# End states of a recurrent unit in one VectorE copy, (a+1) multiplied in ahead of the square root, and ten constant products for four

## The chip, the cores and the metric

The kernel runs on one core of a Trainium2 chip. The metric is the device time of one execution in microseconds, as the median of several runs. Five engines work side by side, each through its own list of instructions in order: TensorE (PE; the loading of its weights is PEld), VectorE (DVE), ScalarE (ACT), GpSimd (POOL) and SyncE (SP, which only issues transfers here). They wait for each other at semaphores.

## The reference

One step of a two-layer backbone over 512 latent and 128 context tokens with 1024 channels. Layer 0 mixes tokens by attention, layer 1 by a bidirectional gated linear recurrence; a SwiGLU feed-forward block follows each. The change touches the recurrence only. For each channel and each direction:

```python
def _rglru_coeffs(xc, w_a, b_a, w_i, b_i, lam):
    ...
    r = jax.nn.sigmoid(jnp.einsum('btnk,nkj->btnj', xb, w_a).reshape(B, T, D) + b_a)
    i = jax.nn.sigmoid(jnp.einsum('btnk,nkj->btnj', xb, w_i).reshape(B, T, D) + b_i)
    log_a = -LRU_C * r * jax.nn.softplus(-lam.astype(jnp.float32))
    a = jnp.exp(log_a)
    b = jnp.sqrt(-jnp.expm1(2.0 * log_a)) * (i * xc)

def _linear_scan(a, b, h0, reverse):
    def step(h, ab):
        a_t, b_t = ab
        h = a_t * h + b_t
        return h, h
```

`xc` is a width-4 convolution over the tokens. The latent scans start from cached states, the context scans from zero. The sum of the forward and the backward states is multiplied by a GeLU gate and goes through the projection `lru_w_out`. The end states of the context scans, one number for each channel and direction, are an output of their own (`new_state_h`).

## The kernel before

Channels lie on the 128 partitions, tokens along the free dimension; 1024 channels make eight blocks f = 0 to 7 of 128. Large products are made in three passes (high part by high part, high by low, low by high: L228, L229, L230 in `some`), each weight tile being split into a high part (`whi`) and a low one (`wlo`, the subtraction of L183 on DVE). In this stage the high parts of the input weights come by a transfer that POOL issues (L179), and DVE can subtract once it has landed.

The recurrent unit is the stage between the two feed-forward blocks, from about 867 to 1014 us. For block f it goes through four functions:

- `lru_a`: the convolution (L1293 on ACT, three L1295 on DVE, into `xc`), four products with the recurrence weights into PSUM tiles `gp` (L1305), four tanh of them on ACT (L1306), giving `tr` for r and `ti` for i, each of 2 directions x 643 tokens; then ti = (ti + 1) * xc (L1307, DVE).
- `lru_b`: from tr, for each direction d, the decay a (L1317, an exponential on ACT) and a tanh that replaces tr (L1318, ACT). Of the new tr the square root is taken (L1319, ACT, both directions at once, after a change of the activation table, L1284, 1.28 us). Then on DVE tr = (a + 1) * tr (L1320) and ti = ti * tr (L1321). ti now holds b.
- `lru_c`: four scans on DVE (L1330; latent and context in each direction), which turn ti into the states h. After each direction POOL copies the one end state of the context scan, a column of h, into the tile `st` (L1332), sixteen copies in all. Then forward and backward states are added on DVE (L1337, L1338).
- `lru_d`: times the gate `gl` (L1343, DVE), the cast to the high part `yhi` (L1348, ACT; named `big` in the profile) and the low part `ylo` (L1350, DVE). For the last block, f = 7, these three are done in two halves.

Beside these, `lru_gate` makes the gates: products on PE, copied out by L1358, or put through GeLU (L1362) straight from PSUM, which frees that PSUM bank for PE's next product.

The stages of different blocks are interleaved: in round t the program writes `lru_a(t)`, `lru_b(t-1)`, `lru_c(t-2)`, `lru_d(t-2)`. On each engine a planner then sets the order: it takes the instructions in the order in which a model of the timeline finds them ready, so that a change of one instruction moves others. On ACT, `turn` chains the calls that need a certain activation table, so that their order is that of the program.

After the stage, `project_halves` multiplies by `lru_w_out`. Five partial products over blocks 0 to 4 are made ahead (L228 to L230), blocks 5, 6, 7 are added as they come (L1052 for yhi, L1054 for ylo), and between block 6 and block 7 `keep` puts products of constants into a PSUM tile that nobody reads (L211, tile `at`): four of 128 x 128. Each shows as two records in the profile. Past block 7 come the remaining five products of the projection, whose weights (`raw` from `in_wlo`) are loaded while the residual `x` is read back from memory (L1371).

Of the kernel before, what the change touches and what calls it, by code (L numbers as in the profile page):

```python
# [12 lines left out]
ALU = mybir.AluOpType  # L13
# [4 lines left out]
KT = D // P  # L18
# [16 lines left out]
LW = 643  # L35
NLT = 10
C0 = 515
# [89 lines left out]
class _Step:  # L127
# [908 lines left out]
    def project_halves(self, w, hi, lo, gk, key, xd):  # L1036
        def out(f, t0, t1, ps):
            self.residual(f, t0, t1, ps, G, True)
            self.nc.sync.dma_start(xd[f * P:f * P + P, t0:t1], self.x[:, f, t0:t1])
        G = self.need(self.gcols, gk)  # L1040
        us = [self.unit(w[f], "m") for f in range(3)]
        early = [(f, t0, t1) for f in range(3) for c, (t0, t1) in enumerate(CH) if c == 0 or f < KT - DEH]
        pss = [(self.ps("mx") if j % 2 else self.pg(False))[:, 0:HT] for j in range(len(early))]
        for (f, t0, t1), ps in zip(early, pss):
            self.some(us[f], hi, lo, t0, t1, ps, range(KT - 3))
        turns = sorted(zip(early, pss), key=lambda e: e[0][1])
        for k in range(KT - 3, KT):
            if k == KT - 1:
                self.keep(self.ps("at"), 4)
            for (f, t0, t1), ps in turns:  # L1050
                for part in us[f]:
                    self.done = self.nc.tensor.matmul(ps, part[:, k], hi[:, k, t0:t1], start=False, stop=False).ins  # L1052
            for (f, t0, t1), ps in turns:
                self.done = self.nc.tensor.matmul(ps, us[f][0][:, k], lo[:, k, t0:t1], start=False, stop=(k == KT - 1)).ins  # L1054
                if k == KT - 1:
                    out(f, t0, t1, ps)
        for f in range(3, KT):
            us.append(self.unit(w[f], "mx"[f % 2]))
            out(f, *CH[0], self.chunk(us[f], hi, lo, *CH[0]))
        self.rt = self.t([P, NTOK], F32, "r", 2)  # L1060
        for c, (t0, t1) in enumerate(CH):
            for f in range(KT - DEH, KT) if c else ():
                out(f, t0, t1, self.chunk(us[f], hi, lo, t0, t1))
                j = f - KT + DEH
                for k in range(max(0, 2 * j - 2), 2 * j) if f < KT - 1 else ():
                    self.first_half(k, key)
            self.stat(t0, t1)
            self.nc.scalar.copy(self.rt[:, t0:t1], self.r[0][:, 0:t1 - t0])
# [241 lines left out]
    def lru_b(self, f, lt, tr, ti):  # L1310
        nc = self.nc
        a = lt()
        nc.vector.tensor_scalar(tr, tr, -1.0, None, ALU.max)
        for d in range(2):
            p2 = self.sp2[:, d * KT + f:d * KT + f + 1]
            n4 = self.sm4[:, d * KT + f:d * KT + f + 1]
            self.turn(AF.Exp, lambda: nc.scalar.activation(a[:, d], tr[:, d], AF.Exp, scale=n4, bias=n4))  # L1317
            self.turn(AF.Exp, lambda: nc.scalar.activation(tr[:, d], tr[:, d], AF.Tanh, scale=p2, bias=p2))  # L1318
        self.turn(AF.Sqrt, lambda: nc.scalar.activation(tr, tr, AF.Sqrt, scale=0.25))  # L1319
        nc.vector.scalar_tensor_tensor(tr, a, 1.0, tr, ALU.add, ALU.mult)  # L1320
        nc.vector.tensor_tensor(ti, ti, tr, ALU.mult)  # L1321
        return a, ti

    def lru_c(self, f, a, h):
        nc = self.nc
        for d in range(2):
            st = self.st[:, d * KT + f:d * KT + f + 1]
            for sl, init in ((slice(0, NLAT), self.col(f"h{d}", f)), (slice(C0, LW), 0.0)):
                hv, av = [t[:, d, sl] if d == 0 else t[:, d, sl][:, ::-1] for t in (h, a)]
                nc.vector.tensor_tensor_scan(hv, av, hv, init, ALU.mult, ALU.add)  # L1330
            e = LW - 1 if d == 0 else C0
            nc.gpsimd.tensor_copy(st, h[:, d, e:e + 1])  # L1332
        y = a[:, 0, 0:NTOK]
        fn, bn = [h[:, d, 0:NLAT].rearrange("p (r c) -> p c r", r=ROWS) for d in range(2)]
        for c0, c1, q0 in ((56, 64, 0), (0, 56, 64)):
            yv = y[:, q0:q0 + (c1 - c0) * ROWS].rearrange("p (c r) -> p c r", r=ROWS)
            nc.vector.tensor_tensor(yv, fn[:, c0:c1], bn[:, c0:c1], ALU.add)  # L1337
        nc.vector.tensor_tensor(y[:, NLAT:NTOK], h[:, 0, C0:LW], h[:, 1, C0:LW], ALU.add)  # L1338
        return y
# [183 lines left out]
```

## Time and profile before

| | |
|---|---|
| Time, median of 3 runs | 1512.68 us (1512.1 to 1513.39) |
| The profiled execution's own time | 1511.01 us |
| Its span, first to last instruction | 1509.2 us |
| PE busy | 1483.2 us, 98% of the span |
| DVE busy | 1062.7 us, 70% |
| ACT busy | 702.5 us, 47% |
| POOL busy | 263.6 us, 17% |
| Mean granted clock of PE | 0.997 |

Rows of the timeline give start, duration, engine, line, operation, the tiles written and read, and in brackets the idle time of that engine just before with what ended it. Rows of the waits give total time, number of times, and the longest. Rows of the windows give the length of the stretch and, for each engine, its busy time and number of instructions; then the granted clock of PE (1.00 is full), the share of the transfer engines in use, and GB/s.

### The profile page before, as it was taken

The numbers are of one execution on the slowest core, as the hardware profiler recorded it, in microseconds if no ns is written. First come the engines' busy times: TensorE is split into PE (matmuls) and PEld (weight loads), VectorE is DVE, ScalarE is ACT, GpSimd is POOL, SyncE is SP. The second block draws the span as 40 slices with busy tenths as digits, with TensorE's granted clock in tenths as the row PEclk, the third lists the DMA queues.
The fourth block names the chain that finished last, engine by engine and source line by source line (L and its number), as shares of the span: only waits on it lengthen the run. The fifth ranks groups of instructions, "written<-read, shape, count | busy, mean of one in ns | idle before, by whom it ended". The sixth has DMA issues, their size and how long they took to land. (4 is left out here: it accounts for less than half of the span.)

```text
span 1509.2 us, 26176 instructions
## 1 busy us (share of the span) xinstructions
PE 1483.2 (98%) x10397; PEld 1436.3 (95%) x10397; DVE 1062.7 (70%) x2007; ACT 702.5 (47%) x1271; POOL 263.6 (17%) x276
## 2 busy tenths in 40 slices
PE   9999999999999999999999999989999999999997
PEld 6999999899999999999999988889999999999997
DVE  5778998679999987434443768886975665565655
ACT  4676766664332123312321568874644342424243
POOL 0112133101111110000000013230331323232211
PEclk9999999999999999999999999999999999999999
DMA  9645765445666663222222544325242231313211
GB/s 375 177 145 160 187 190 171 118 154 183 185 187 200 204 199 123 62 86 83 66 75 83 160 131 122 105 73 199 80 140 87 67 113 56 112 57 100 69 57 71
DMA packets 72331, 196.66 MB, mean 130 GB/s; under 512 B 8048, under 2 KB 24592, under 8 KB 72080
## 3 DMA queue, kind: packets, MB, share of 16 engines
q1 hardware_dynamic: 57392, 142.32, 29.8%
q0 software_dynamic: 14240, 51.98, 11.4%
q8 instruction: 82, 1.34, 0.4%
q10 hardware_dynamic: 576, 0.68, 0.1%
q14 instruction: 41, 0.34, 0.1%
HBM read 179.48 MB, written 8.92 MB: 125 GB/s over the span
## 5 line engine op out<-in xcount | busy, mean ns | idle before, releaser
L229 PE MATMUL mm<-big,whi 128*128 128x320 f32 (+3 forms) x1224 | 380.4, 311 | 0.8 <-DVE big L1350 0.5
L228 PE MATMUL mm<-big,whi 128*128 128x320 f32 (+3 forms) x1224 | 378.5, 311 | 2.7 <-ACT gl L1362 1.2
L230 PE MATMUL mm<-big,wlo 128*128 128x320 f32 (+3 forms) x1224 | 377.7, 309 | 0.3 <-DVE wlo L183 0.3
L228 PEld LDWEIGHTS mm<-big,whi 128*128 128x128 f32 x1224 | 229.8, 188 | 4.9 <-ACT gl L1362 1.5
L229 PEld LDWEIGHTS mm<-big,whi 128*128 128x128 f32 x1224 | 230.1, 188 | 2.7 <-DVE big L1350 0.8
L230 PEld LDWEIGHTS mm<-big,wlo 128*128 128x128 f32 x1224 | 230.4, 188 | 1.7 <-DVE wlo L183 0.5
L257 DVE SCALAR_TENSOR_TENSOR mprod<-mraw,csb 128x1024 f32<-128x1024 f32 x160 | 195.7, 1223 | 10.4 <-DMA mraw<-in_wm 9.9
L598 DVE SCALAR_TENSOR_TENSOR x<-mm,G,x 128x320 f32<-128x320 f32 (+2 forms) x192 | 77.8, 436 | 81.7 <-PE mm L230 81.3
L181 ACT CAST whi<-raw 128x1024 fp32r<-128x1024 f32 (+1 forms) x71 | 73.9, 1040 | 112.0 <-PE mm L229 63.5
L183 DVE TENSOR_TENSOR wlo<-raw,whi 128x1024 fp32r<-128x1024 f32 (+1 forms) x87 | 105.1, 1208 | 28.4 <-ACT whi L181 12.8
L229 PE MATMUL mm<-big,whx 128*128 128x320 f32 (+3 forms) x348 | 108.1, 311 | 0.0
L230 PE MATMUL mm<-big,wlx 128*128 128x320 f32 (+3 forms) x348 | 107.8, 310 | 0.0
L228 PE MATMUL mm<-big,whx 128*128 128x320 f32 (+3 forms) x348 | 107.6, 309 | 0.0
L253 POOL DMA_DIRECT2D mraw<-in_wm x80 | 43.1, 539 | 352.8 <-DVE mprod L257 265.4
L229 PE MATMUL mx<-big,whi 128*128 128x320 f32 (+3 forms) x281 | 87.0, 309 | 0.0
L230 PE MATMUL mx<-big,wlo 128*128 128x320 f32 (+3 forms) x281 | 86.8, 309 | 0.0
L228 PE MATMUL mx<-big,whi 128*128 128x320 f32 (+3 forms) x281 | 86.8, 309 | 0.0
L181 ACT CAST whx<-raw 128x1024 fp32r<-128x1024 f32 (+1 forms) x40 | 41.1, 1029 | 85.2 <-PE mm L229 46.7
L229 PE MATMUL mx<-big,whx 128*128 128x320 f32 (+3 forms) x260 | 80.4, 309 | 0.0
L230 PE MATMUL mx<-big,wlx 128*128 128x320 f32 (+3 forms) x260 | 80.3, 309 | 0.0
L228 PE MATMUL mx<-big,whx 128*128 128x320 f32 (+3 forms) x260 | 80.1, 308 | 0.0
L1348 ACT CAST whi<-raw 128x1024 fp32r<-128x1024 f32 (+1 forms) x41 | 41.3, 1007 | 70.5 <-PE mm L229 44.5
(363 smaller groups left out, 3753.3 us busy)
## 6 DMA issues: line engine op xcount, KB each, us to landing
raw<-in_gu SPq DMA_DIRECT2D x88, 512.0 KB, 3.5
mraw<-in_wm POOLq DMA_DIRECT2D x80, 512.0 KB, 3.9
raw<-in_dn SPq DMA_DIRECT2D x24, 512.0 KB, 3.6
sw<-in_wm SPq DMA_DIRECT2D x16, 512.0 KB, 10.7
raw<-in_wqk SPq DMA_DIRECT2D x16, 512.0 KB, 4.9
raw<-in_wi SPq DMA_DIRECT2D x16, 512.0 KB, 3.5
whi<-in_wi POOLq DMA_DIRECT2D x16, 512.0 KB, 4.0
raw<-in_dn SPq DMA_DIRECT2D x16, 448.0 KB, 3.3
```

Of the source, the lines that this page charges most:

```text
L181: nc.scalar.copy(hi, raw)
L183: nc.vector.tensor_tensor(lo, raw, hi.bitcast(F32), ALU.subtract)
L228: nc.tensor.matmul(ps, hi[:, k], xhi[:, k, s], start=(k == 0), stop=False)
L229: nc.tensor.matmul(ps, hi[:, k], xlo[:, k, s], start=False, stop=False)
L230: self.done = nc.tensor.matmul(ps, lo[:, k], xhi[:, k, s], start=False, stop=(k == last)).ins
L253: nc.gpsimd.dma_start(w, self.i["wm"][l * 6 + j - 2, f])
L257: nc.vector.scalar_tensor_tensor(prod, w, 1.0, self.csb[:, s], ALU.mult, ALU.mult, accum_out=out[:, s, f:f + 1])
L598: self.nc.vector.scalar_tensor_tensor(xs, ps[:, a - t0:b - t0], G[:, s, f:f + 1], xs, ALU.mult, ALU.add)
L1348: self.nc.scalar.copy(hi, v)
```

## The change

Three edits, all in the recurrent unit and the projection behind it:

1. In `lru_b` the factor (a + 1) goes into ti, before the square root is there, and no longer into tr, after it. The two exponentials are written one after the other, then the DVE product, then the two tanh.
2. In `lru_c` the sixteen POOL copies of one column each become eight DVE copies of two columns each, one for a block, after its four scans.
3. `project_halves` puts ten products of constants between block 6 and block 7, where there were four.

```diff
             if k == KT - 1:
-                self.keep(self.ps("at"), 4)
+                self.keep(self.ps("at"), 10)
...
         for d in range(2):
-            p2 = self.sp2[:, d * KT + f:d * KT + f + 1]
             n4 = self.sm4[:, d * KT + f:d * KT + f + 1]
             self.turn(AF.Exp, lambda: nc.scalar.activation(a[:, d], tr[:, d], AF.Exp, scale=n4, bias=n4))
+        nc.vector.scalar_tensor_tensor(ti, a, 1.0, ti, ALU.add, ALU.mult)
+        for d in range(2):
+            p2 = self.sp2[:, d * KT + f:d * KT + f + 1]
             self.turn(AF.Exp, lambda: nc.scalar.activation(tr[:, d], tr[:, d], AF.Tanh, scale=p2, bias=p2))
         self.turn(AF.Sqrt, lambda: nc.scalar.activation(tr, tr, AF.Sqrt, scale=0.25))
-        nc.vector.scalar_tensor_tensor(tr, a, 1.0, tr, ALU.add, ALU.mult)
         nc.vector.tensor_tensor(ti, ti, tr, ALU.mult)
         return a, ti
...
         for d in range(2):
-            st = self.st[:, d * KT + f:d * KT + f + 1]
             for sl, init in ((slice(0, NLAT), self.col(f"h{d}", f)), (slice(C0, LW), 0.0)):
...
-            e = LW - 1 if d == 0 else C0
-            nc.gpsimd.tensor_copy(st, h[:, d, e:e + 1])
+        ends = bass.AP(tensor=h.tensor, offset=h[:, 0, LW - 1:LW].offset, ap=[list(h.ap[0]), [C0 + 1, 2]])
+        nc.vector.tensor_copy(self.st.rearrange("p (d k) -> p k d", d=2)[:, f], ends)
```

The lines of the changed kernel: the exponentials are L1316, the DVE product with (a + 1) is L1317, the tanh L1320, the root L1321, the product with the root L1322; the copy of the end states is still L1332. All other lines keep their numbers.

In the order of instructions, three places matter to what follows. The first is DVE at the end of the stage, from the sums of block 6 to the first scan of block 7 (a scan is called SCALAR_TENSOR_TENSOR here; `lt` are tr, ti and a of the blocks). Before:

```order
L1338 TENSOR_TENSOR lt_10644<-lt_10455 128x128
L183 TENSOR_TENSOR wlo_10921<-raw_10918,whi_10920 128x1024
L1343 TENSOR_TENSOR lt_10644<-lt_10644,gl_10724 128x640
L1350 TENSOR_TENSOR big_9510<-lt_10534,big_9509 128x640
L1350 TENSOR_TENSOR big_9510<-lt_10644,big_9509 128x640
L1320 SCALAR_TENSOR_TENSOR lt_10624<-lt_10787,lt_10624 128x1286
L1321 TENSOR_TENSOR lt_10625<-lt_10625,lt_10624 128x1286
L1330 SCALAR_TENSOR_TENSOR lt_10625<-lt_10787,cols_61,lt_10625 128x512
```

The same place in the changed kernel:

```order
L1332 COPY st_74<-lt_10451 128x2
L1338 TENSOR_TENSOR lt_10639<-lt_10451 128x128
L1343 TENSOR_TENSOR lt_10639<-lt_10639,gl_10718 128x640
L1317 SCALAR_TENSOR_TENSOR lt_10620<-lt_10781,lt_10620 128x1286
L183 TENSOR_TENSOR wlo_10913<-raw_10910,whi_10912 128x1024
L1350 TENSOR_TENSOR big_9510<-lt_10530,big_9509 128x640
L1350 TENSOR_TENSOR big_9510<-lt_10639,big_9509 128x640
L1322 TENSOR_TENSOR lt_10620<-lt_10620,lt_10619 128x1286
L1330 SCALAR_TENSOR_TENSOR lt_10620<-lt_10781,cols_61,lt_10620 128x512
```

The product with (a + 1) of block 7 now stands ahead of the weight subtraction L183 and of two low parts L1350; behind the root only one product is left before the scans. A copy of end states stands between the sums of each block.

The second is ACT at the same time, from the first exponential of block 7 to its root. Before:

```order
L1317 ACTIVATE lt_10787<-lt_10624,l_sm_387_2014 128x643
L181 CAST whi_10920<-raw_10918 128x1024
L1358 COPY gl_10807<-mm_10840 128x256
L1348 CAST big_9509<-lt_10534 128x640
L1318 ACTIVATE lt_10624<-lt_10624,l_sp_386_2012 128x643
L1317 ACTIVATE lt_10787<-lt_10624,l_sm_387_2014 128x643
L1318 ACTIVATE lt_10624<-lt_10624,l_sp_386_2012 128x643
L1284 ACT_TABLE_LOAD
L1348 CAST big_9509<-lt_10644 128x640
L1319 ACTIVATE lt_10624<-lt_10624 128x1286
```

In the changed kernel:

```order
L1316 ACTIVATE lt_10781<-lt_10619,l_sm_387_2014 128x643 x2
L181 CAST whi_10912<-raw_10910 128x1024
L1358 COPY gl_10800<-mm_10833 128x256
L1348 CAST big_9509<-lt_10530 128x640
L1320 ACTIVATE lt_10619<-lt_10619,l_sp_386_2012 128x643 x2
L1284 ACT_TABLE_LOAD
L1348 CAST big_9509<-lt_10639 128x640
L1321 ACTIVATE lt_10619<-lt_10619 128x1286
```

The same ten instructions stand there, the second exponential three instructions earlier.

The third is DVE in the middle of the stage, where block 1 passes its root, block 4 its convolution and block 2 its L1307. Before:

```order
L1295 SCALAR_TENSOR_TENSOR xc_10109<-xr_1597_9517,cols_61,xc_10109 128x643
L1350 TENSOR_TENSOR big_9510<-lt_9818,big_9509 128x640
L1295 SCALAR_TENSOR_TENSOR xc_10109<-xr_1597_9517,cols_61,xc_10109 128x643 x2
L1320 SCALAR_TENSOR_TENSOR lt_9739<-lt_9915,lt_9739 128x1286
L183 TENSOR_TENSOR wlo_10307<-raw_10304,whi_10306 128x1024
L1321 TENSOR_TENSOR lt_9740<-lt_9740,lt_9739 128x1286
```

In the changed kernel:

```order
L1307 SCALAR_TENSOR_TENSOR lt_9836<-lt_9836,xc_9830 128x1286
L1317 SCALAR_TENSOR_TENSOR lt_9740<-lt_9915,lt_9740 128x1286
L1350 TENSOR_TENSOR big_9510<-lt_9818,big_9509 128x640
L1295 SCALAR_TENSOR_TENSOR xc_10107<-xr_1597_9517,cols_61,xc_10107 128x643 x3
L1322 TENSOR_TENSOR lt_9740<-lt_9740,lt_9739 128x1286
L183 TENSOR_TENSOR wlo_10304<-raw_10301,whi_10303 128x1024
```

Here too the product with (a + 1) moved ahead of the convolution, and the product with the root ahead of the weight subtraction. On POOL the sixteen L1332 are gone, and thirteen L179 follow each other with nothing between. On PE the order is the same up to block 5; from there the products L1305 of blocks 5, 6 and 7 stand two to ten instructions earlier, the last two of block 7 where they stood.

## The prediction

> **What bounds the kernel now.** I read the first rows of the page, then PE's waits, then the stage of the recurrent unit in the timeline. The page:
>
> ```profile
> PE 1483.2 (98%) x10397; PEld 1436.3 (95%) x10397; DVE 1062.7 (70%) x2007; ACT 702.5 (47%) x1271; POOL 263.6 (17%) x276
> ```
>
> PE has work in 98% of the span, so an edit on DVE, ACT or POOL is worth only what it takes from PE's waits, or from the time in which PE is clocked down. PE's waits (total, times, longest):
>
> ```profile
> PE mm L1052 <- ACT big L1348: 5.5, 1, 5.5
> PE mm L228 <- ACT gl L1362: 1.2, 1, 1.2
> PE mm L230 <- DVE wlo L183: 0.3, 1, 0.3
> ```
>
> The longest of the whole kernel, 5.5 us, is at the place of the change: PE has done all it can and waits for block 7 of the recurrent unit. In one-microsecond windows (length, then busy time of PE, PEld, DVE, ACT, POOL, then the clock):
>
> ```profile
> 1008.00:1009.00 1.00, 0.86 (x8) 0.66 (x6) 0.96 (x2) 0.00 (x0) 0.00 (x0) 1.00 0.00 0
> 1011.00:1012.00 1.00, 0.00 (x0) 0.00 (x0) 1.00 (x2) 0.00 (x0) 0.74 (x1) 0.59 0.02 8
> 1012.00:1013.00 1.00, 0.00 (x0) 0.00 (x0) 1.00 (x3) 0.00 (x0) 0.78 (x1) 0.50 0.00 0
> 1017.00:1018.00 1.00, 1.00 (x6) 1.00 (x5) 1.00 (x1) 0.00 (x0) 0.00 (x0) 0.50 1.04 399
> 1018.00:1019.00 1.00, 1.00 (x8) 1.00 (x8) 0.67 (x3) 0.67 (x1) 0.00 (x0) 1.00 1.01 407
> ```
>
> The wait costs twice: PE stops at 1008.86, its clock halves at about 1011.2, 2.3 us later, and it stays at 0.50 until about 1018, some 3.8 us into the new work. The chain that ends the wait, in the timeline:
>
> ```profile
> 1004.61 1.28 ACT L1319 ACTIVATE lt<-lt 128x1286 f32<-128x1286 f32 x1
> 1005.93 1.50 DVE L1320 SCALAR_TENSOR_TENSOR lt<-lt,lt 128x1286 f32<-128x1286 f32 x1 [0.36 <-ACT lt L1319]
> 1007.46 1.50 DVE L1321 TENSOR_TENSOR lt<-lt,lt 128x1286 f32<-128x1286 f32 x1
> 1007.80 1.05 PE L211 MATMUL at<-ident,ones 128*128 128x128 f32 x8
> 1008.99 1.28 DVE L1330 TENSOR_TENSOR_SCAN lt<-lt,cols,lt 128x512 f32<-128x512 f32 x1
> 1013.80 0.86 ACT L1348 CAST big<-lt 128x320 fp32r<-128x320 f32 x2 [5.85 <-DVE lt L1343]
> 1014.31 0.64 PE L1052 MATMUL mm<-big,whi 128*128 128x320 f32 x1 [5.45 <-ACT big L1348]
> ```
>
> From the root to PE's restart DVE is the chain: two products, four scans, sums, the gate. Everything after 1014.31 is PE's again.
>
> **The product out of the chain.** L1320 starts at 1005.93 and L1321 at 1007.46: 1.53 us leave the chain, if DVE is free when the root ends. It is: in the changed order the product stands behind the sums of block 6, where both exponentials are long done, and DVE had 0.74 and 0.36 us of idle time from there to the root, plus 2.30 us just after block 7's L1307:
>
> ```profile
> 1004.74 0.82 DVE L1350 TENSOR_TENSOR big<-lt,big 128x640 fp32r<-128x640 f32 x1 [0.74 <-ACT big L1348]
> 993.23 1.50 DVE L1320 SCALAR_TENSOR_TENSOR lt<-lt,lt 128x1286 f32<-128x1286 f32 x1 [2.30 <-ACT lt L1319]
> ```
>
> Block 6's own product fills that 2.30 us, so DVE reaches the end of block 6 about 1.5 us sooner and spends that on block 7's product. Queued behind it is the weight subtraction L183, for which PE waited 0.3 us; it may end up to 0.8 us later, but PE then only uses up a part of its 5.5 us.
>
> **The copy into the chain.** One copy of 128x2 enters DVE's queue between the sums and the gate. No such copy is in the trace; below it lies the smallest write, above it the reciprocal of the same shape:
>
> ```profile
> L1380 DVE MEMSET mhalf<- 128x1 f32 x1 | 0.1, 59 | 0.8 <-PEq L1515 0.8
> L883 DVE RECIPROCAL sm<-sm 128x2 f32<-128x2 f32 x8 | 1.3, 161 | 2.4 <-ACT S L882 2.4
> ```
>
> I take the row of its shape, 0.16 us (0.06 to 0.16). The chain gains 1.53 - 0.16 = 1.37 us. The other seven copies, 1.1 us in all, lie in DVE's idle time. The POOL copies cost PE nothing where they were, but they hold up the weight transfers that POOL issues, and those DVE:
>
> ```profile
> 932.65 5.31 POOL L1332 COPY st<-lt 128x1 f32<-128x1 f32 x1 [0.47 <-DVE lt L1330]
> 938.21 0.53 POOL L179 DMA_DIRECT2D whi<-in_wi  x1 [0.25 <-PE mm L230]
> 942.01 1.23 DVE L183 TENSOR_TENSOR wlo<-raw,whi 128x1024 fp32r<-128x1024 f32 x1 [4.10 <-issue]
> ```
>
> The transfer went out at 938.21, just behind a copy, and DVE stood for 4.10 us until it had landed.
>
> **An earlier start of the tail.** The root of block 7 hangs on ACT, and ACT on PE. These rows show how:
>
> ```profile
> 919.86 1.48 DVE L1307 SCALAR_TENSOR_TENSOR lt<-lt,xc 128x1286 f32<-128x1286 f32 x1
> 921.38 0.92 ACT L1293 ACTIVATE xc<-xr,cols 128x643 f32<-128x643 f32 x1 [0.93 <-DVE lt L1307]
> 927.02 0.38 ACT L1362 ACTIVATE gl<-mm 128x256 f32<-128x256 f32 x1
> 927.46 0.44 PE L228 MATMUL mm<-big,whi 128*128 128x384 f32 x1 [1.25 <-ACT gl L1362]
> 970.40 0.80 ACT L1306 ACTIVATE lt<-gp,l_hb 128x643 f32<-128x643 f32 x1 [0.28 <-PE gp L1305]
> 1007.21 0.74 ACT L1362 ACTIVATE gl<-gl 128x640 f32<-128x640 f32 x1
> ```
>
> From 970.40 to 1007.95 ACT shows no idle time (45 instructions): what lets it start, PE's product for block 6, sets the root. PE in turn lost 1.25 us at 927.46, on a PSUM bank that the GeLU at 927.02 had to free; that GeLU was late because ACT's convolution waited 0.93 us for DVE's L1307. In the changed order DVE takes block 1's product with the root right after the root instead of behind 1.50 us of L1320, and the scans, the sums and L1307 follow sooner by about that. Then 0.93 us of ACT's wait goes, and two hand-overs from exponential to tanh (0.97 us apart where the tanh overwrites what the exponential reads, 0.83 us where it doesn't) give 0.2 us more:
>
> ```profile
> 986.62 0.94 ACT L1317 ACTIVATE lt<-lt,l_sm 128x643 f32<-128x643 f32 x1
> 987.59 0.93 ACT L1318 ACTIVATE lt<-lt,l_sp 128x643 f32<-128x643 f32 x1
> 988.42 0.91 ACT L1317 ACTIVATE lt<-lt,l_sm 128x643 f32<-128x643 f32 x1
> ```
>
> So PE is 0.93 + 0.2 = 1.1 us earlier from 927 on. The planner also sets block 6's products about five matmuls of 384 columns earlier, 0.7 us at the spacing of 0.145 us for 320 columns in the rows below. And ACT itself, back to back from there, has three more pairs of exponentials and tanh without the hand-over, about 0.3 us. Together the root of block 7 comes 1.1 + 0.7 + 0.3 = 2.1 us earlier. I hold this term from 0 (some other wait takes over) to 2.5 us. DVE must keep pace; it does, by the 1.5 us per block that it no longer spends between root and scans.
>
> PE restarts, then, 1.37 + 2.1 = 3.5 us earlier, at 1010.8.
>
> **The constants.** Four products took 1.05 us, so six more take 1.57. PE reaches them about 1.1 us earlier than before, or as late as before with the later L183, and ends them at 1009.5 to 1011.1, ahead of the restart in either case. They cost nothing, and the gap is 1.3 to 1.7 us, where the clock took 2.3 us of gap to halve. If PE got to them late, all 1.57 us would be paid.
>
> **The clock.** With the gap that short the clock stays at 1.00. Fifteen matmuls of block 7 ran from 1014.31 to 1018.27 at half clock; the same fifteen of block 6 took from 1005.61 to 1007.80:
>
> ```profile
> 1005.61 0.31 PE L1052 MATMUL mm<-big,whi 128*128 128x320 f32 x1
> 1018.27 0.30 PE L228 MATMUL mx<-big,whx 128*128 128x320 f32 x1
> ```
>
> That is 3.96 - 2.19 = 1.77 us. Not all of it is to be had. Past the restart the transfer engines are full (1.01 above) with the residual and the weights, and those don't run faster with PE's clock:
>
> ```profile
> 1026.07 1.05 ACT L181 CAST whi<-raw 128x1024 fp32r<-128x1024 f32 x1 [2.20 <-DMA raw<-in_wlo]
> 1027.16 1.23 DVE L183 TENSOR_TENSOR wlo<-raw,whi 128x1024 fp32r<-128x1024 f32 x1 [2.76 <-ACT whi L181]
> 1029.09 0.31 PE L230 MATMUL mx<-big,wlo 128*128 128x320 f32 x1
> ```
>
> This weight's low part is done at 1028.39, and PE uses it at 1029.09: 0.70 us of slack. The transfers start with the restart, so I count 0.7 us of the 1.77, and PE waits there for the rest. Its bounds are 0.7 and 1.77.
>
> The Trainium skill's page "TensorE: Matmul & The Clock Gate", section "What's actually happening", says that the clock is halved after an idle window of about 3.4 us that runs freely, and freed after a busy one of the same length. Here the row differs: 2.3 us sufficed to halve it, and 3.8 us to free it. By the page a gap of 2.3 to 3.4 us would often be safe; by the row it isn't. With my gap of 1.3 to 1.7 us both keep the clock up, and the sum is the same by either; if the tail came late and the gap were 3 us, the page would still give the 0.7 us, and the row would not.
>
> **The sum.** 1.37 + 2.1 + 0.7 = 4.2 us. Against the profiled execution's 1511.01 us that is 1506.8; that execution lies 1.67 us below the median of the runs, 1512.68, and I predict the median: 1508.5 us. What a measurement of this kernel can tell from no change is about 0.2%, 3.0 us.
>
> **Rivals.**
>
> Only the chain gains. ACT's tail starts no earlier, since another wait (a cast for DVE's gate product, a weight) fills the place: 1.37 + 0.7 = 2.1 us, 1510.6. For it: ACT waited 0.28 us for PE at 970.40, so PE's gain must arrive there whole. Against it: every product of block 6 and 7 moves earlier or stays. Chance 0.20.
>
> The gain is swallowed behind the restart. Between 1015 and 1030 the transfer engines are full, and if a weight behind the first is late as well, or the new order of the projection's pieces opens a wait, PE gives back most of the 4.2 us: about 1512. For it: the slack of 0.70 us. Against it: after 1050 no row of PE's waits names a transfer. Chance 0.12.
>
> The clock halves all the same, since the gate counts activity over a longer stretch: 1.37 + 2.1 = 3.5 us, 1509.2. Against it: PE is at full clock to the end of the constants. Chance 0.06.
>
> Slower: DVE's queue. In four blocks (3, 4, 7 and 0) the product with (a + 1) stands directly ahead of a weight subtraction L183, and waits there for both exponentials. PE waited 0.3 us for such a subtraction once, so somewhere the slack is nothing. If it is nothing in all four, PE loses 4 x 1.50 = 6.0 us, against 2.1 us won at the end: 1516.6. It decides from the point at which more than 2.8 us of these 6.0 reach PE outside its last wait. Against it: the exponentials end before DVE gets there wherever DVE had idle time, as the 4.10 and 2.30 us above. Chance 0.07.
>
> My own forecast has the remaining 0.55; its own range, with the tail from 1.2 to 2.5 us and the clock from 0.7 to 1.77, is 1507.0 to 1509.5.
>
> **How the numbers follow.** The range reaches from 1507.2 to 1511.3: it leaves out the slower case, most of the swallowed one and the best corner. Faster by more than 0.2% means under 1509.65 us: nearly all of my forecast (0.52), most of the halved clock (0.04) and a little of the others (0.03), 0.59. Slower is the DVE queue, 0.07. Within 0.2% is the rest, 0.34.
>
> **What would show it.** PE's wait at the first L1052 of block 7 should fall from 5.45 us to 1 to 2 us, behind twenty records of L211 in place of eight; the clock should read 1.00 in every window from 1005 to 1020; L1322 should follow the root within 0.1 us; the wait of 1.25 us on the GeLU should be nearly gone; and a new wait of about 1 us on L183 should stand some 13 us behind the restart. I'd be wrong if ACT showed idle time in the tail between block 6's tanh and block 7's root, if PE's waits for L183 grew before 1000 us, or if the distance from restart to the end of the program grew instead of shrinking by 0.7.

## The result: 0.3% faster

| | kernel before | changed kernel |
|---|---|---|
| Median of 7 runs | 1512.93 us (1511.64 to 1513.66) | 1506.83 us (1505.57 to 1511.03) |
| Profiled execution, its span | 1511.01 us, 1509.2 us | 1508.43 us, 1506.4 us |
| Mean granted clock of PE | 0.997 | 0.998 |

The ratio is 0.9969 (95% interval 0.9959 to 0.9979): faster by 0.31%, 4.7 us of the 1512.68 us that the prediction started from. Two later sets of runs of the same kernel, each beside its own runs of the kernel before, gave 0.9963 (0.9951 to 0.9976) and 0.9967 (0.9954 to 0.9979).

The first row of the changed kernel's page, and PE's waits between 860 and 1060 us:

```profile
PE 1483.1 (98%) x10409; PEld 1435.1 (95%) x10409; DVE 1063.1 (71%) x2015; ACT 701.6 (47%) x1271; POOL 222.5 (15%) x260
```

```profile
PE mm L1052 <- ACT big L1348: 1.5, 1, 1.5
PE mm L230 <- DVE wlo L183: 0.2, 1, 0.2
```

The wait at block 7 fell from 5.5 to 1.5 us, and the 1.2 us on the GeLU are gone. POOL lost 41 us of busy time, 39 of them its sixteen copies. The windows around the restart (length, busy time of PE, PEld, DVE, ACT, POOL, then the clock):

```profile
1008.00:1009.00 1.00, 1.00 (x12) 1.00 (x10) 1.00 (x4) 0.00 (x0) 0.00 (x0) 1.00 0.00 0
1010.00:1011.00 1.00, 0.25 (x1) 0.25 (x2) 0.88 (x3) 0.76 (x2) 0.46 (x1) 1.00 0.00 0
1017.00:1018.00 1.00, 1.00 (x9) 1.00 (x8) 1.00 (x2) 0.00 (x0) 0.00 (x0) 1.00 1.04 410
```

The clock reads 1.00 in all three, where in the kernel before it read 0.50 from 1011.2 to 1018 us. The timeline of the same stage, first the row that I use as the stage's zero in both kernels (block 0's first gate tanh), before and after:

```profile
869.07 0.80 ACT L1306 ACTIVATE lt<-gp,l_hb 128x643 f32<-128x643 f32 x1 [2.95 <-PE gp L1305]
```

```profile
869.27 0.80 ACT L1306 ACTIVATE lt<-gp,l_hb 128x643 f32<-128x643 f32 x1 [2.95 <-PE gp L1305]
...
918.47 1.51 DVE L1307 SCALAR_TENSOR_TENSOR lt<-lt,xc 128x1286 f32<-128x1286 f32 x1
...
926.04 0.39 ACT L1362 ACTIVATE gl<-mm 128x256 f32<-128x256 f32 x1
...
968.69 0.80 ACT L1306 ACTIVATE lt<-gp,l_hb 128x643 f32<-128x643 f32 x1 [0.46 <-PE gp L1305]
...
1002.48 1.27 ACT L1321 ACTIVATE lt<-lt 128x1286 f32<-128x1286 f32 x1
1003.79 1.50 DVE L1322 TENSOR_TENSOR lt<-lt,lt 128x1286 f32<-128x1286 f32 x1 [0.35 <-ACT lt L1321]
...
1006.85 2.39 PE L211 MATMUL at<-ident,ones 128*128 128x128 f32 x20
1009.42 0.19 DVE L1332 COPY st<-lt 128x2 f32<-128x2 f32 x1
1010.24 0.86 ACT L1348 CAST big<-lt 128x320 fp32r<-128x320 f32 x2 [4.43 <-DVE lt L1343]
1010.75 0.42 PE L1052 MATMUL mm<-big,whi 128*128 128x320 f32 x1 [1.51 <-ACT big L1348]
```

From that zero to PE's restart the kernel before takes 145.24 us, the changed one 141.48: 3.76 us less. The root comes 2.33 us earlier (133.21 against 135.54), and root to restart is 8.27 us where it was 9.70.

The two spans differ by 2.8 us only. Restart to end grew, from 494.9 to 495.65 us. By ACT's `snap` copies, which follow PE, the changed kernel stood 4.65 us ahead at 1102 us and 2.99 us ahead from 1233 us on: 1.66 us were given back, most of it in two places of the last feed-forward part:

```profile
1157.94 0.83 ACT L1348 CAST whi<-raw 128x768 fp32r<-128x768 f32 x1 [2.61 <-DMA raw<-in_dn]
1175.74 0.41 PE L1111 MATMUL mx<-xt,wuh 128*128 128x320 f32 x1 [0.45 <-ACT snap L1117]
1232.32 0.41 PE L229 MATMUL mm<-big,whi 128*128 128x320 f32 x1 [0.36 <-DVE big L1350]
1233.47 0.41 PE L1111 MATMUL mx<-xt,wuh 128*128 128x320 f32 x1 [0.59 <-ACT snap L1117]
```

A weight of the down projection landed late for ACT. As I read the rows, the next weight's transfer, POOL's sums of it, ACT's casts and the `snap` copy came late behind it, and PE waited for that.

### The profile page after: what moved, and what is told of

Read it like the earlier page. It is cut to its first block, busy times and chain, and to the rows that moved or that the text cites. A ratio compares the mean times of both kernels' runs of the same rounds, so it can differ in the third digit from the quotient of the medians.

```text
span 1506.4 us, 26172 instructions
## 1 busy us (share of the span) xinstructions
PE 1483.1 (98%) x10409; PEld 1435.1 (95%) x10409; DVE 1063.1 (71%) x2015; ACT 701.6 (47%) x1271; POOL 222.5 (15%) x260
## 3 DMA queue, kind: packets, MB, share of 16 engines
q8 instruction: 82, 1.34, 0.4%
## 5 line engine op out<-in xcount | busy, mean ns | idle before, releaser
L183 DVE TENSOR_TENSOR wlo<-raw,whi 128x1024 fp32r<-128x1024 f32 (+1 forms) x87 | 105.2, 1209 | 24.7 <-ACT whi L181 11.9
```

The costliest lines, as they stand in the source:

```text
L183: nc.vector.tensor_tensor(lo, raw, hi.bitcast(F32), ALU.subtract)
```

## The experiments

All times from zero to restart are measured from the row of block 0's first gate tanh, since the stage itself starts at another time in each profile (869.03 to 871.34 us). The columns up to the stage come from one profiled execution of each kernel. In the last column each row is set against its own runs of the kernel before, on the same chip.

| Kernel | zero | root | restart | zero to restart | time as a ratio to the kernel before |
|---|---|---|---|---|---|
| before | 869.07 | 1004.61 | 1014.31 | 145.24 | |
| changed | 869.27 | 1002.48 | 1010.75 | 141.48 | 0.9969 (0.9959 to 0.9979) |
| changed, second profile | 869.14 | 1002.38 | 1010.63 | 141.49 | 0.9963 (0.9951 to 0.9976) |
| changed, third profile | 869.03 | 1002.27 | 1010.53 | 141.50 | 0.9967 (0.9954 to 0.9979) |
| changed, four constants | 869.23 | 1002.42 | 1010.65 | 141.42 | 0.9972 (0.9961 to 0.9983) |
| the same, second profile | 869.67 | 1002.90 | 1011.14 | 141.47 | 0.9969 (0.9957 to 0.9980) |
| product alone | 870.64 | 1005.94 | 1014.12 | 143.48 | 0.9988 (0.9978 to 0.9998) |
| DVE copy alone | 870.80 | 1006.71 | 1016.47 | 145.67 | 1.0004 (0.9995 to 1.0013) |
| changed, and POOL's copies too | 869.58 | 1008.66 | 1016.90 | 147.32 | 0.9988 (0.9979 to 0.9997) |
| product in block 7 alone | 869.19 | 1003.02 | 1012.11 | 142.92 | 0.9987 (0.9976 to 0.9998) |
| product in blocks 0 to 6 alone | 870.04 | 1009.17 | 1018.88 | 148.84 | 1.001 (1.000 to 1.002) |
| before, twenty constants | 871.19 | 1006.88 | 1016.57 | 145.38 | 0.9995 (0.9986 to 1.0004) |
| changed, root of block 7 split | 871.34 | 1004.56 | 1012.36 | 141.02 | 0.9965 (0.9952 to 0.9977) |
| and first half of block 7 first | 869.82 | 1003.05 | 1009.88 | 140.06 | 0.9972 (0.9961 to 0.9983) |

### The product in block 7 alone

```diff
+        if f == KT - 1:
+            nc.vector.scalar_tensor_tensor(ti, a, 1.0, ti, ALU.add, ALU.mult)
+        for d in range(2):
+            p2 = ...                            # both tanh behind both exponentials
         self.turn(AF.Sqrt, ...)
-        nc.vector.scalar_tensor_tensor(tr, a, 1.0, tr, ALU.add, ALU.mult)
+        if not (f == KT - 1):
+            nc.vector.scalar_tensor_tensor(tr, a, 1.0, tr, ALU.add, ALU.mult)
```

> The kernel before, with both exponentials ahead of both tanh in every block, and the product with (a + 1) ahead of the root in block 7 alone; in the other blocks it stays behind the root. POOL copies and four constant products as before. My theory (the chain of block 7 and an earlier tail are two separate terms): the product leaves block 7's chain, 1.53 us, and the two shorter hand-overs on ACT give some 0.5 us, so PE restarts at about 1012.3 us where it restarted at 1014.31; the gap after the four products stays over 2.3 us, so the clock halves as before. Gain 2.0 us, 1511 where the kernel before takes 1513. DVE's product in blocks 0 to 6 still delays the convolution of the next block, so PE's wait of 1.25 us on the GeLU at 927 stays. Rival (the order alone does it: all of the 2.1 us of the tail come from the planner's order and ACT's hand-overs, nothing from DVE's product in the earlier blocks): restart at 1010.7, gain 3.6 us.

Measured: 2.32 us off the stage, where I expected 2.0, but not by my two terms. The root came 1.71 us earlier and not 0.5, root to restart fell by 0.61 us (to 9.09) and not by 1.53.

```profile
925.95 0.39 ACT L1366 ACTIVATE gl<-mm 128x256 f32<-128x256 f32 x1
...
1003.02 1.28 ACT L1322 ACTIVATE lt<-lt 128x1286 f32<-128x1286 f32 x1
...
1009.02 0.80 DVE L1354 TENSOR_TENSOR big<-lt,big 128x640 fp32r<-128x640 f32 x1
...
1012.11 0.42 PE L1052 MATMUL mm<-big,whi 128*128 128x320 f32 x1 [0.34 <-ACT big L1352]
```

(Lines behind the edit are four higher here.) The GeLU ran at 925.95 and PE's 1.25 us behind it were gone, though DVE's product of block 1 still stood behind the root: with both exponentials first the planner let ACT do both tanh ahead of the convolution that had waited for DVE. So in this one profile the order of ACT's calls, with what the planner moved for it, does most of what I had put down to DVE. The chain lost 0.71 us of its gain to block 6's low part, which now stood between block 7's scans and sums (1009.02). The gap that I expected to stay over 2.3 us was 0.34 us: PE had already waited 0.68 and 1.11 us for block 6, its constants ended at 1011.76, and the clock stayed at 1.00.

### The product in blocks 0 to 6 alone

The same edit with `f < KT - 1` as the condition.

> The kernel before, with both exponentials ahead of both tanh in every block, and the product with (a + 1) ahead of the root in blocks 0 to 6; in block 7 it stays behind the root, in the chain. POOL copies and four constant products as before. My theory: PE's wait of 1.25 us on the GeLU goes, and the root of block 7 comes 2.1 us earlier, at 1002.5 where it was at 1004.61; from the root to the restart the chain is as long as before (9.70 us), restart at 1012.2, clock halved as before, gain 2.1 us. Rival (only the chain gains): the root comes less than 0.5 us earlier, restart at 1014, gain under 0.5 us.

Measured: the stage 3.60 us longer instead of 2.1 shorter. Root to restart stayed at 9.71 us, as expected; the root came 3.59 us later. Rows of the timeline about block 4's scans (the copy is L1336 here):

```profile
966.32 4.30 POOL L1336 COPY st<-lt 128x1 f32<-128x1 f32 x1 [0.47 <-DVE lt L1334]
969.70 0.87 DVE L1295 SCALAR_TENSOR_TENSOR xc<-xr,cols,xc 128x643 f32<-128x643 f32 x1
970.56 0.53 POOL L179 DMA_DIRECT2D whi<-in_wi  x1
974.39 1.23 DVE L183 TENSOR_TENSOR wlo<-raw,whi 128x1024 fp32r<-128x1024 f32 x1 [3.83 <-issue]
976.52 3.85 PE L1305 MATMUL gp<-xc,gw 128*128 128x512 f32 x8 [3.90 <-issue]
```

One column, 128x1, keeps POOL 4.30 us, until 970.62; DVE's unbroken run of work ends at 970.57. Behind the copy stands a weight transfer; DVE's subtraction waits for it, the last tap of the next block's convolution stands behind that subtraction, and PE waits 3.90 us for the convolution. In the kernel before the order was the other way round, and nothing waited:

```profile
964.73 0.53 POOL L179 DMA_DIRECT2D whi<-in_wi  x1 [8.64 <-PE mm L230]
969.12 1.02 POOL L1332 COPY st<-lt 128x1 f32<-128x1 f32 x1 [3.85 <-DVE lt L1330]
```

Neither of my theories had this wait in it. The profiled execution took 1517.08 us where the median of the twelve was 1513.31; its clock was halved at 977.3 and again at 1018.3 us, and how far the other executions had the same wait is not on record.

### The product alone, in all blocks

The first edit of the change without the other two.

> The changed kernel's first part alone: the product ahead of the root in every block; POOL copies and four constant products as before. My theory: both terms, 1.53 and 2.1 us, restart at 1010.7. The tail with its four products ends at about 1007.8, so the gap is 2.9 us, and since the row of the kernel before shows the clock halved 2.3 us after the last matmul, it halves again and all or most of the 1.77 us of the clock are lost: gain 3.6 us, 1.0 to 1.8 us less than the changed kernel's. Rival by the Trainium skill, page 'TensorE: Matmul & The Clock Gate', section 'What's actually happening' (an idle window of about 3.4 us that runs freely): the clock stays at 1.00 in most executions, gain 5 us, as the changed kernel's. Rival on the copies (POOL's copies hold up weight transfers): the gain is 1 us or more below that of the changed kernel with four products, the next run, which differs in the copies alone.

Measured: 1.76 us off the stage, not 3.6. The same wait, shorter:

```profile
967.14 1.98 POOL L1333 COPY st<-lt 128x1 f32<-128x1 f32 x1 [0.47 <-DVE lt L1331]
969.07 0.53 POOL L179 DMA_DIRECT2D whi<-in_wi  x1
974.96 2.40 PE L1305 MATMUL gp<-xc,gw 128*128 128x512 f32 x8 [1.74 <-issue]
1014.12 0.41 PE L1052 MATMUL mm<-big,whi 128*128 128x320 f32 x1 [2.85 <-ACT big L1349]
```

Root to restart is 8.18 us: the chain's gain is whole (9.70 before). The rest of the loss is the root, 0.24 us earlier where the changed kernel has 2.33. The clock was halved here from 1015.42 to 1018.83 us, as I expected; the rival with the clock at 1.00 doesn't show in this profile. The rival on the copies holds, by 2.06 us of the stage and by the medians: 1510.31 us here, 1508.46 in the next run, which differs in the copies alone.

### Four constants in the changed kernel

```diff
-                self.keep(self.ps("at"), 10)
+                self.keep(self.ps("at"), 4)
```

> The changed kernel with four constant products where it has ten. My theory: restart at 1010.7 as in the changed kernel, tail's end 1.57 us sooner, at 1007.7, a gap of 3.0 us; the clock is halved from about 1010.0 to 1014 and the fifteen matmuls of block 7 take nearly 4 us where they took 2.2: gain 1.0 to 1.8 us less than the changed kernel's. Rival by the Trainium skill's page named above (a free window of 3.4 us): no halved clock in most executions and the changed kernel's gain. The same gain as the run before within 0.5 us if the copies cost nothing; over 1 us more if POOL's copies held transfers up.

Measured: 3.82 us off the stage, no wait at L1305, time as the changed kernel's. With DVE's copy the weight leaves POOL at 963.68, 94.45 us behind the zero; with the product alone it was 98.43. The gap at the restart is 2.83 us, and the clock is halved in this profile (windows of 0.4 us):

```profile
963.68 0.53 POOL L179 DMA_DIRECT2D whi<-in_wi  x1 [8.63 <-PE mm L230]
1010.65 0.63 PE L1052 MATMUL mm<-big,whi 128*128 128x320 f32 x1 [2.83 <-ACT big L1348]
```

```profile
1010.40:1010.80 0.40, 0.15 (x1) 0.15 (x1) 0.28 (x2) 0.40 (x2) 0.00 (x0) 0.66 0.00 0
1013.60:1014.00 0.40, 0.40 (x4) 0.40 (x3) 0.40 (x1) 0.00 (x0) 0.00 (x0) 0.57 1.03 410
```

A mean of 0.66 puts the halving at 1010.53, one of 0.57 the freeing at 1013.94: 3.41 us. It cost 3.29 / 2 = 1.64 us of PE's work, and the time does not show them: 0.9972 here, 0.9969 for the changed kernel.

### Second and third profiles, and the two counts side by side

The changed kernel, unchanged, was run again in two further sets, the second time beside the kernel with four constants.

> The changed kernel once more, for a second profile. In its first profile PE restarted 3.56 us earlier, stood 4.65 us ahead of the kernel before from 1102 to 1154 us, and 2.99 us ahead from 1232 us to the end: 1.66 us were given back in two places of the last feed-forward part, at 1175 (PE waits for ACT's snap) and 1232 (for DVE's split and the snap). Theory A (the late transfers of those places are chance): this profile does not give back 0.8 us at either place, and keeps over 4 us to the end. Theory B (the weights there are paced by transfers and POOL's sums, not by PE, so whoever comes over 3.8 us ahead waits): the same two waits again, 0.8 us each within 0.3, and about 3 us at the end. Time 4 to 6 us under the kernel before in both, since the timed runs said so.

> The changed kernel with four constant products, beside the next run on the same chip. Gap of 2.8 us at the restart: the clock is halved in the profile if some 2 us of it fall into one of the clock's windows. Theory A (the 1.6 us of the halved clock reach the end): 1.0 to 1.6 us slower than the next run. Theory B (taken back in the last feed-forward part): the same within 0.5 us.

> The changed kernel, for the comparison with the run before. Restart 141.5 us behind the first gate tanh, clock 1.00 around it. Theory A: 1.0 to 1.6 us faster than the run before; theory B: the same within 0.5 us. Two of two profiles showed ACT waiting 2.6 us for a transfer of the down projection 148 us behind the restart, and 0.8 us of PE's lead lost some 17 us later; if that is the kernel's own pace, a third profile shows it again.

Measured: the stage is the same to 0.02 us in all three profiles of the changed kernel. The late weight of the down projection is not:

```profile
1158.38 0.83 ACT L1348 CAST whi<-raw 128x768 fp32r<-128x768 f32 x1 [2.60 <-DMA raw<-in_dn]
```

```profile
1155.91 0.83 ACT L1348 CAST whi<-raw 128x768 fp32r<-128x768 f32 x1 [0.93 <-DMA raw<-in_dn]
```

The second profile has it, the third hasn't. So it is no fixed pace of the weights, and neither theory on it stands whole. Counted from the restart this cast starts at 147.19, 147.75 and 145.38 us; why the transfer lands up to 2.4 us later in some executions is open. Restart to end was 495.65, 494.97 and 494.17 us, against 494.9 in the one profile of the kernel before.

With four constants the second profile has the same gap as the first, and no halved clock:

```profile
1011.14 0.42 PE L1052 MATMUL mm<-big,whi 128*128 128x320 f32 x1 [2.82 <-ACT big L1348]
```

```profile
1010.80:1011.20 0.40, 0.06 (x1) 0.06 (x1) 0.28 (x2) 0.40 (x2) 0.05 (x1) 1.00 0.00 0
1011.20:1011.60 0.40, 0.40 (x3) 0.40 (x4) 0.40 (x2) 0.40 (x2) 0.00 (x0) 1.00 0.10 21
```

Two executions of one program, one halved and one not: restart to end 494.55 and 493.96 us. In this pair 0.59 us of the 1.64 us is left at the end, but the three profiles of the changed kernel, all at full clock, differ by 1.48 us there. The medians were 1507.59 us with four constants (6 runs) and 1507.88 with ten (5 runs): theory B, no difference that these runs can tell.

### Twenty constants in the kernel before

```diff
-                self.keep(self.ps("at"), 4)
+                self.keep(self.ps("at"), 20)
```

> The kernel before with twenty constant products where it has four: the clock term alone. They end at about 1013.0, 1.3 us ahead of the restart, which stays at 1014.3, so the clock stays at 1.00. Theory A (what the clock saves reaches the end): restart to end falls by 0.7 to 1.8 us from the 494.9 us of the kernel before, gain 0.7 to 1.8 us. Theory B (the 1.77 us are taken back by weights behind it): restart to end stays within 0.4 us of 494.9, gain under 0.4 us.

Measured: 0.9995 (0.9986 to 1.0004), between 2.1 us gained and 0.6 lost. The stage is as before (145.38), the gap 1.87 us and the clock 1.00 at the restart, yet restart to end is 497.1 us:

```profile
1100.32 0.42 PE L1168 MATMUL mm<-xt,whx 128*128 128x320 f32 x1 [1.77 <-DVE g L1130]
```

This wait stands in every kernel (1.2 to 2.0 us); here the clock was halved behind it, from 1101.1 to 1104.5 us, and in this execution, at 1515.51 us the longest of the eleven, that took back what the constants had saved. The run doesn't tell the two theories apart.

### The DVE copy alone

The second edit of the change without the other two.

> The kernel before with the DVE copy in place of POOL's two: the second part alone. In the kernel before, no transfer that PE or DVE waited for stood behind a POOL copy near the end of the stage (block 5's weight went out at 964.73 us, its copies came at 969.12). Theory A (the copies cost only where the moved product has pushed a weight transfer behind them): from the stage's first gate tanh to PE's restart 145.2 us as in the kernel before, within 0.4 us; time within 0.5 us of it. Theory B (the copies cost 2 us in any order): 143.3 us, gain 2 us.

Measured: no gain, 1.0004, and 0.43 us more in the stage, of which 0.4 is PE's wait on the GeLU (1.64 us where it was 1.25). Theory A, to 0.03 us of the stage and 0.1 us of the time more than it allowed.

```profile
929.57 0.45 PE L228 MATMUL mm<-big,whi 128*128 128x384 f32 x1 [1.64 <-ACT gl L1361]
1016.47 0.63 PE L1052 MATMUL mm<-big,whi 128*128 128x320 f32 x1 [5.43 <-ACT big L1347]
```

### The changed kernel with POOL's copies beside it

```diff
         nc.vector.tensor_copy(self.st.rearrange("p (d k) -> p k d", d=2)[:, f], ends)
+        for d, e in ((0, LW - 1), (1, C0)):
+            nc.gpsimd.tensor_copy(self.st_pool[:, d * KT + f:d * KT + f + 1], h[:, d, e:e + 1])
```

> The changed kernel, and beside its DVE copy POOL's two copies of the kernel before, into columns that nobody reads: 16 copies more. The run with the product alone had a weight transfer that left POOL at 969.07 us, behind a copy, where it left at 963.68 without them, and a wait of 1.74 us on PE behind it. Theory A (POOL's copies hold up the transfers that are queued behind them on POOL): that wait returns, 143.3 to 143.6 us from the first gate tanh to the restart where the changed kernel takes 141.5, and the time is 1.5 to 2.5 us over the changed kernel's. Theory B (the run with the product alone was slower only for the planner's order of PE's products): 141.5 us within 0.3, no wait, no difference.

Measured: theory A, and more of it. 147.32 us, with PE's wait of 4.03 us; time 1510.4 us where the changed kernel took 1507.88 on the same chip.

```profile
966.07 4.41 POOL L1334 COPY st_pool<-lt 128x1 f32<-128x1 f32 x1 [0.47 <-DVE lt L1330]
970.42 0.53 POOL L179 DMA_DIRECT2D whi<-in_wi  x1
976.31 3.90 PE L1305 MATMUL gp<-xc,gw 128*128 128x512 f32 x8 [4.03 <-issue]
```

Nobody reads these columns. Counted from the zero, the weight leaves POOL at 100.84 us instead of 94.45, and 4.41 us of the difference are the second copy. The profiled execution took 1514.19 us, the longest of the eleven; five of the eleven, 1507.95 to 1508.73, lie within 0.9 us of the changed kernel's median. So the 5.8 us by which this stage is longer than the changed kernel's is one execution's price, and 2.5 us is the price by the medians. The same copy took 1.98, 4.30 and 4.41 us in the profiles of three kernels; what it took in the other executions is not on record.

### Shortening what is left of the wait

The first kernel splits root and product of block 7 by direction; the second, on top of it, puts the long scans, the sums of 320 tokens and their gate product ahead of the rest.

```diff
-        self.turn(AF.Sqrt, lambda: nc.scalar.activation(tr, tr, AF.Sqrt, scale=0.25))
-        nc.vector.tensor_tensor(ti, ti, tr, ALU.mult)
+        for d in (slice(0, 1), slice(1, 2)) if f == KT - 1 else (slice(0, 2),):
+            self.turn(AF.Sqrt, lambda: nc.scalar.activation(tr[:, d], tr[:, d], AF.Sqrt, scale=0.25))
+            nc.vector.tensor_tensor(ti[:, d], ti[:, d], tr[:, d], ALU.mult)
```

> The changed kernel with root and product of block 7 split by direction, so that DVE's product starts when half of the root (0.65 us) is done. DVE's chain is the bound of the restart, so it starts 0.6 us earlier and costs one more instruction, some 0.06 us: restart 0.5 us earlier than the changed kernel's, 1010.2, wait at it 1.0 us where it was 1.51. Gain over the changed kernel 0.5 us. Rival (ACT sets the restart, by the cast or the GeLU of block 7): restart unchanged within 0.15 us.

> The run before this one, and in block 7 the two long scans, the sums of the first 320 tokens and their gate product stand ahead of the two short scans, the other sums and the copy. The first cast then waits for 0.32 + 0.32 + 0.4 + 0.27 us less on DVE: restart 1.2 us earlier than in the run before, at about 1009.2, where the ten constant products end, so PE's wait there is under 0.3 us. The second half of block 7 comes as late as before, or 0.1 us later, so PE may wait there: it uses the second half 0.9 us behind the restart, and has 0.6 us of slack in the changed kernel. Restart and the second wait together: 0.6 us won over the run before, 1.1 us over the changed kernel. Rival: PE's wait goes whole to the second half, and nothing is won.

Measured: the split took 0.46 us off the stage, as expected (141.02). The second brought PE to block 7 after 140.06 us without a wait, and the wait moved on:

```profile
1012.08 0.41 PE L1052 MATMUL mx<-big,whi 128*128 128x320 f32 x1 [0.51 <-ACT big L1375]
1014.29 0.42 PE L230 MATMUL mx<-big,wlx 128*128 128x320 f32 x1 [0.71 <-DVE wlx L183]
```

Neither beats the changed kernel by anything that the runs can tell: 0.9965 and 0.9972 beside 0.9963 on the same chip. Half a microsecond is below what a set of five to seven runs shows here.

## Why the prediction was right, and where it wasn't

**The size.** I predicted 4.2 us off. The ratios of the three sets of runs give 4.7, 5.6 and 5.0 us; by the first, 1508.0 us from the median that I started from, against 1508.5. The median of the first seven runs, 1506.83, lies 0.4 us below my lower end, with the kernel before 0.25 us higher in that set than in the runs I had been shown. What the extra 0.5 to 1.4 us over my sum are, beyond the tail's 0.2, is not settled.

**The product out of the chain: right.** L1322 starts 0.04 us behind the root's end, and root to restart fell by 1.43 us for my 1.37. The product alone, with root to restart at 8.18 us, shows it by itself.

**The copy into the chain: right in size, wrong in worth.** The row is 0.19 us, but the next instruction starts 0.07 us behind its start; my lower bound was 0.06. But I costed edit 2 as a price of 0.16 us with nothing on the other side. It is what makes edit 1 pay: without it the stage gains 1.76 us, with it 3.8, and with POOL's copies put back beside it the stage of the one profile is 2.1 us longer than in the kernel before. I had named the mechanism (copies hold up the transfers behind them) and then priced it by the order of the kernel before, where it cost nothing, without asking which transfers the moved product would put behind a copy. The forecast came out right only because the three edits came together; for edit 1 alone my sum would have been off by 1.8 us. Two effects that I hadn't priced, the hold-up that edit 1 brings and its removal by edit 2, cancelled: that part was luck. And at the place that I quoted for it I was wrong: without any copy the transfer leaves at 937.21 where it left at 938.21, still released by PE's use of the old weight, and DVE still waits 3.89 us:

```profile
937.21 0.53 POOL L179 DMA_DIRECT2D whi<-in_wi  x1 [10.09 <-PE mm L230]
```

```profile
941.20 1.23 DVE L183 TENSOR_TENSOR wlo<-raw,whi 128x1024 fp32r<-128x1024 f32 x1 [3.89 <-issue]
```

**The earlier tail: right in size (2.33 us for 2.1), half wrong in its cause.** Its steps came as summed: counted from the zero, the GeLU is 1.18 us earlier (1.1 predicted), block 6's tanh that sets ACT going (968.69 for 970.40) 1.91 us (1.8) and the root 2.33 us. DVE's L1307 does come 1.6 us sooner from the zero (918.47 us for 919.86) and ACT's wait for it is gone, as I said. But the kernel with the product moved in block 7 alone has the GeLU 1.19 us earlier and the root 1.71 us, with DVE's product of block 1 still behind the root. The order of exponentials and tanh, with what the planner makes of it, is therefore enough for most of the term; I had given it 0.5 us. That is one profile, and the planner moved other instructions in it as well.

**The restart: 3.76 us earlier in the stage, 3.5 predicted.** PE's first wait at L1052 is 1.51 us, twenty records of L211 stand ahead of it, and the clock reads 1.00, all as foretold.

**Slips in the sum that did no harm.** The six more constants took 1.34 us (2.39 for twenty records, 1.05 for eight), not 1.57. The latest end that I allowed them, 1011.1, lies behind my own restart at 1010.8, so "ahead of the restart in either case" didn't follow; they ended at 1009.24. Five matmuls of 384 columns are 0.9 us at the 0.17 us at which such matmuls follow each other in the kernel before; I had taken the spacing of 320 columns. And the second exponential of block 7 moved up by four places in ACT's order, not by three.

**The clock: it stayed up as foretold, its worth at the end is not shown, and its rule was wrong.** At the restart nearly all of the 1.77 us was there: the matmul that came 14.78 us behind the restart comes 13.26 us behind it (13.83 and 13.24 in the other two profiles). The two profiles with four constants, one with a halved clock and one without, differ by 0.97 us at that matmul (14.60 and 13.63), by 0.76 us at ACT's first `snap` copy (92.54 and 91.78 us behind the restart, where the three with ten constants have 91.39 to 92.13) and by 0.59 us at the end. I had counted 0.7 us for the end. But there the three profiles of the changed kernel stand -0.75, -0.1 and +0.7 us from one of the kernel before with no difference in the clock among them, and the medians with four and ten constants show nothing. The wait of 1 us on L183 that was to take the rest back is 0.4 us in one profile and absent in two. By my own test (restart to end growing) the first profile spoke against the step, the third for it. So the share of edit 3 in the gain is not shown.

My reading that 2.3 us of gap halve the clock falls. The halved stretches measure 3.41 us (four constants; product alone, 1015.42 to 1018.83) or twice that (6.83 in the kernel before, 1011.18 to 1018.01), and a gap of 2.8 us halved it in one execution (2.83) and not in another (2.82). That fits a window of 3.41 us that runs on its own and doesn't start with the gap: in the run with blocks 0 to 6 alone the two halvings, at 977.32 and 1018.28 us, lie twelve such windows apart. The Trainium skill's page "TensorE: Matmul & The Clock Gate", section "What's actually happening", gives a free-running window of about 3.4 us; the traces agree. In the kernel before, PE was still at work for 1.09 us of the window that halved it (the 3.41 us up to 1011.18), so a gap need not fill one. How much of a window must be idle these runs don't say.

**The rivals.** The slower one, DVE's queue, did not show: PE had no wait for L183 in the stage before 1000 us, as in the kernel before; the one behind it, at 1001.63, is 0.2 us where it was 0.3. Behind the restart, from ACT's `snap` copies at 1102 us to those at 1233, the three profiles of the changed kernel gave back 1.66, 0.96 and 0.65 us of their lead, so swallowing took a part of the gain and not most of it. That only the chain gains is excluded by the root's 2.33 us. The rival that I lacked is POOL's copies in front of the transfers that the moved product pushes behind them.

## What to carry to other kernels

Price an edit in the order that the other edits make, not in the order of the profile: copies of one column that cost nothing before were worth some 2 us by the medians, and almost 6 us of the stage in one profile, once another instruction had moved. A small copy on an engine that also issues transfers can hold those up: here one column kept POOL for 4.41 us ahead of a weight for which PE then stood idle, so look in its queue for what stands behind it. Where the start of a stage shifts from run to run, measure the stage from its own first instruction: that agreed to 0.02 us here, where spans of the same kernel differed by 1.7.

## What the runs showed of the hardware

- POOL's copy of 128x1 took 0.63 to 6.47 us in the kernel before (median 1.03), and the two behind which PE waited 3.90 and 4.03 us ended with DVE's run of work: 970.62 against 970.57 us with the product in blocks 0 to 6, and 970.48 against 970.44 in the kernel with both copies. A pause isn't always needed: with the product alone the copy of 1.98 us ended at 969.12, 0.04 us behind the end of one DVE instruction, when the next had started at 969.00. The Trainium skill's page "SBUF — State Buffer", section "Who interferes with whom", says that a DVE instruction with two SBUF inputs contends with a GpSimd instruction that reads SBUF. These rows fit it in the main, though the run of work that ended at 970.57 also held an instruction with one such input (L1313), and nothing here separated the port from other causes.
- To free the clock takes more than to keep it: in the run with blocks 0 to 6 alone the clock, halved at 1018.28, stayed so through a window in which PE stood idle for 0.60 us, and came back at 1025.10, two windows later. At the restart no gap under 1.9 us halved it (1.08 to 1.87 us in six profiles). The wait of 1.77 us at L1168 did, once, so the length of a gap alone doesn't decide it.
- The stage began between 869.0 and 871.3 us, and that goes with the clock near the start, 1.00 in the first 30 us of the one and 0.89 in the other (granted clock third from the right; the kernel before, then twenty constants):

```profile
0.00:30.00 30.00, 27.31 (x159) 18.80 (x159) 17.30 (x33) 13.82 (x22) 2.14 (x8) 1.00 0.95 365
```

```profile
0.00:30.00 30.00, 26.03 (x141) 17.74 (x142) 16.52 (x31) 14.03 (x22) 2.13 (x8) 0.89 0.95 367
```

That is 2 us of difference between executions, as much as half of the change's gain, and it has nothing to do with the change.
